# A two-layer decoder on one core: the FFN's down projection in two pairs of column blocks, with mixed pairs of row tiles

## The chip, the cores and the metric

The kernel runs on 1 core of one Trainium2 chip. The metric is the device time of one execution in microseconds (us). The kernel before takes 2395.1 us, the median of three runs (2394.01 to 2396.98).

## The reference

A state-space layer and a sliding-window attention layer, each followed by a SwiGLU feed-forward network (FFN), all in float32, 256 tokens of 2048 features. Around every part stand RMS norms. What this case changes is the FFN and the norm behind it, which run once in each of the two layers:

```
def rmsnorm(x, w):
    xf = x.astype(jnp.float32)
    xf = xf * lax.rsqrt(jnp.mean(xf * xf, axis=-1, keepdims=True) + EPS)
    return (xf * w.astype(jnp.float32)).astype(x.dtype)

def swiglu(u, w_gate, w_up, w_down):
    return (jax.nn.silu(u @ w_gate) * (u @ w_up)) @ w_down
...
        ffn = swiglu(rmsnorm(h, g[2]), ffn_w_gate[layer], ffn_w_up[layer], ffn_w_down[layer])
        h = h + rmsnorm(ffn, g[3])
```

`w_gate` and `w_up` are 2048 x 5632, `w_down` is 5632 x 2048.

## The kernel before

Every float32 product is made of three matmuls of fp32r tiles. A weight tile is loaded to `raw`, ACT casts it to a high half `whi` (line 113), DVE subtracts that from the raw tile and gets a low half `wlo` (line 114). The activations are kept as two halves in the same way. A product is then high x high, high x low and low x high, accumulated in one PSUM bank of 128 x 512.

The class `Weights` streams all weights in the order of one list, `specs`. It has five raw buffers and four buffers for converted halves; `next` converts up to three tiles ahead of the one that TensorE uses, and loads raw tiles ahead of that. A plain raw tile holds two row tiles of 128 x 512; its use is 12 matmuls (two row tiles, two token tiles, three matmuls). All loads of weights are issued on SP's queue.

Gate and up run in 11 units of 512 columns. From the second unit on, three of the eight pairs of row tiles are mixed. Gate and up stand side by side as a 2 x 2 block matrix (two row tiles, two column blocks), the two token tiles and two row tiles make a 2 x 2 block of activations, and their product is made with 7 products instead of 8. This needs sums of weight tiles (`_mixed`, lines 77 to 91, on DVE) and differences of activations (`mixed_x`, lines 624 to 635, once for each layer, kept in `sx`). The weights of a mixed pair come in four parts: "a" (two tiles as loaded), "13" (first sum, lines 87), "24" (second sums, lines 89 and 90, written into the raw tile in place) and "g" (one tile as loaded). The seven products collect in banks p1 to p7. When the last mixed pair is done, lines 696 to 700 recombine p1, p5, p6 and p7 into four stored terms, and lines 705 add them to the banks p2, p4, p3 and up1 at the unit's end; Silu and two products make a block of the hidden activations, which TensorE transposes during the next unit (line 641).

The down projection runs in `mix_stage` as four column blocks of 512, one after the other, with 22 plain raw tiles each. Behind a block ACT sums its squares and DVE multiplies by the norm's weights `gpost`, in the bank; all four blocks stay in the eight banks. The last block's final tiles are held (two in layer 0, four in layer 1) and run first for token tile 0, then for token tile 1. GpSimd makes the factor of the norm from the squares (line 240), and line 547 adds the scaled block to the residual `h`. `h` leaves the chip's SBUF for DRAM during the units (`spill_h`) and comes back through `fetch_h`, on GpSimd's queue, at the start of down.

The order on each engine is made by the framework's list scheduler from the order of the calls; `high_priority` moves a group ahead, `keep_in_program_order` pins it. The order on an engine is fixed when the kernel runs.

## Time and profile before

| | us |
|---|---|
| median of three runs | 2395.1 |
| the profiled execution | 2395.28 |
| its span, first to last instruction | 2393.6 |
| TensorE busy | 2371.8 |
| DVE busy | 1808.4 |
| ACT busy | 1322.2 |
| GpSimd busy | 92.0 |

Busy time of TensorE is a union of overlapping matmuls: a row of 0.39 us may start 0.23 us after the one before. In the lines of groups the first number after the bar is busy time in us, the second the mean duration in ns, then idle time of the engine before these instructions and what ended it. In a timeline the columns are start and duration in us, engine, line, operation, out<-in, shapes and count; in brackets stands the idle time before, with what ended it.

### The profile page before, as it was taken

How to read it: one execution, taken by the hardware profiler on the slowest of the kernel's cores; microseconds unless marked ns; L12 is line 12 of the kernel's file. 1: busy time of each engine (PE TensorE's matmuls, PEld its weight loads, DVE VectorE, ACT ScalarE, POOL GpSimd, SP SyncE). 2: the span in 40 equal slices, each digit the busy share in tenths (PEclk: the TensorE clock that was granted, in tenths of full speed). 3: DMA queues.
4: the chain of work that ended last, by engine and by line, in shares of the span. 5: the costliest groups of instructions: out<-in, count | busy, mean ns of one | idle time of the engine just before them, and what ended most of it. 6: DMA issues, size and time to landing. Idle time of an engine off the chain costs nothing.

```text
span 2393.6 us, 31662 instructions
## 1 busy us (share of the span) xinstructions
PE 2371.8 (99%) x11630; PEld 1963.9 (82%) x11630; DVE 1808.4 (76%) x2513; ACT 1322.2 (55%) x1867; POOL 92.0 (4%) x74
## 2 busy tenths in 40 slices
PE   9999999999999999999999999999999999999998
PEld 8888888888878888888888878777888888788887
DVE  6998878875567999999744468865899998894444
ACT  6666766664455555555544457755555555554443
POOL 2500100010000000000000000000000000000000
PEclk9999999999999999999999999999999999999999
DMA  7666666657665566565766664435565665566664
GB/s 224 182 202 191 192 186 193 187 174 245 194 199 193 181 202 211 187 213 175 270 193 194 194 192 151 129 123 184 189 210 181 207 211 178 200 230 225 193 194 142
DMA packets 287483, 462.19 MB, mean 193 GB/s; under 512 B 19024, under 2 KB 117584, under 8 KB 285536
## 3 DMA queue, kind: packets, MB, share of 16 engines
q1 hardware_dynamic: 285856, 451.39, 59.3%
q0 software_dynamic: 1184, 8.45, 0.9%
q8 instruction: 91, 1.49, 0.3%
q14 instruction: 64, 0.52, 0.1%
q10 hardware_dynamic: 288, 0.33, 0.0%
HBM read 453.76 MB, written 6.36 MB: 192 GB/s over the span
## 4 chain that ended last, share of the span: by engine, by line
PE 95%; ACT 2%; DVE 2%; issue 1%; DMA 0%; POOL 0%; DVEq 0%; SPq 0%; ACTq 0%; POOLq 0%
PE bank L286 14%; PE bank L345 12%; PE bank L346 12%; PE bank L344 12%; PE bank L669 11%; PE bank L670 11%; PE bank L668 11%; PE bank L291 8%; PE bank L641 1%; ACT whi L113 1%; DVE wlo L114 1%; PE bank L940 1%; PE bank L1116 1%; PE bank L1159 1%; PE bank L406 1%
## 5 line engine op out<-in xcount | busy, mean ns | idle before, releaser
L114 DVE TENSOR_TENSOR wlo<-raw,whi 128x1024 fp32r<-128x1024 f32 (+1 forms) x845 | 988.6, 1184 | 471.5 <-ACT whi L113 465.0
L113 ACT CAST whi<-raw 128x1024 fp32r<-128x1024 f32 (+1 forms) x845 | 853.7, 1022 | 790.4 <-PE bank L346 413.8
L286 PE MATMUL bank<-xx,whi 128*128 128x512 f32 (+1 forms) x1488 | 523.5, 397 | 0.0
L291 PE MATMUL bank<-xx,wlo 128*128 128x256 f32 (+1 forms) x1488 | 416.1, 285 | 0.0
L668 PE MATMUL bank<-whi,xx 128*128 128x512 f32 x980 | 385.2, 393 | 0.5 <-ACT whi L113 0.5
L669 PE MATMUL bank<-wlo,xx 128*128 128x512 f32 x980 | 382.2, 390 | 1.8 <-DVE wlo L114 1.8
L670 PE MATMUL bank<-whi,xx 128*128 128x512 f32 x980 | 382.3, 390 | 0.0
L286 PEld LDWEIGHTS bank<-xx,whi 128*128 128x128 f32 (+1 forms) x1488 | 276.6, 188 | 61.3 <-issue 0.4
L291 PEld LDWEIGHTS bank<-xx,wlo 128*128 128x128 f32 (+1 forms) x1488 | 280.3, 188 | 11.3 <-issue 7.0
L344 PE MATMUL bank<-whi,hh 128*128 128x512 f32 x704 | 274.2, 390 | 0.0
L346 PE MATMUL bank<-whi,hl 128*128 128x512 f32 x704 | 274.0, 389 | 0.0
L345 PE MATMUL bank<-wlo,hh 128*128 128x512 f32 x704 | 273.9, 389 | 0.0
L669 PEld LDWEIGHTS bank<-wlo,xx 128*128 128x128 f32 x980 | 184.1, 188 | 43.0 <-DVE wlo L114 5.4
L668 PEld LDWEIGHTS bank<-whi,xx 128*128 128x128 f32 x980 | 184.1, 188 | 38.1 <-ACT whi L113 0.9
L670 PEld LDWEIGHTS bank<-whi,xx 128*128 128x128 f32 x980 | 184.0, 188 | 37.9
L346 PEld LDWEIGHTS bank<-whi,hl 128*128 128x128 f32 x704 | 132.2, 188 | 27.5
L345 PEld LDWEIGHTS bank<-wlo,hh 128*128 128x128 f32 x704 | 132.2, 188 | 27.3
L344 PEld LDWEIGHTS bank<-whi,hh 128*128 128x128 f32 x704 | 132.2, 188 | 27.2
L113 ACT CAST whi<-t 128x1024 fp32r<-128x1024 f32 x60 | 63.2, 1054 | 90.6 <-DVE t L87 73.9
L344 PE MATMUL bank<-whi,yh 128*128 128x512 f32 x256 | 100.1, 391 | 0.0
L346 PE MATMUL bank<-whi,yl 128*128 128x512 f32 x256 | 99.7, 390 | 0.0
L345 PE MATMUL bank<-wlo,yh 128*128 128x512 f32 x256 | 99.6, 389 | 0.0
(215 smaller groups left out, 2868.1 us busy)
## 6 DMA issues: line engine op xcount, KB each, us to landing
raw<-in_ffn_w_down_dram SPq DMA_DIRECT2D x176, 512.0 KB, 4.8
raw<-in_ssm_w_in_dram SPq DMA_DIRECT2D x161, 512.0 KB, 4.4
raw<-in_ffn_w_gate_dram SPq DMA_DIRECT2D x116, 512.0 KB, 5.1
raw<-in_ffn_w_up_dram SPq DMA_DIRECT2D x116, 512.0 KB, 5.0
raw<-in_ssm_w_out_dram SPq DMA_DIRECT2D x64, 512.0 KB, 4.8
raw<-in_ffn_w_gate_dram SPq DMA_DIRECT2D x120, 256.0 KB, 3.8
raw<-in_ffn_w_up_dram SPq DMA_DIRECT2D x120, 256.0 KB, 4.2
raw<-in_attn_w_q_dram SPq DMA_DIRECT2D x32, 512.0 KB, 3.4
```

Source lines behind the costliest of these rows:

```text
L113: self.pin(nc.scalar.copy(hi[:], src))
L114: self.pin(nc.vector.tensor_tensor(lo[:], src, hi[:].bitcast(F32), ALU.subtract))
L286: nc.tensor.matmul(o, wh, xx[:, kt, :, :].rearrange("p a t -> p (a t)"), start=(kt == 0), stop=(kt == kts - 1))
L291: nc.tensor.matmul(o[:, :T], wl, xx[:, kt, 0, :], start=False, stop=False)
L344: nc.tensor.matmul(o, sh, wh, start=(kt == 0), stop=False)
L345: nc.tensor.matmul(o, sh, wl, start=False, stop=False)
L346: nc.tensor.matmul(o, sl, wh, start=False, stop=(kt == kts - 1))
L406: nc.tensor.matmul(o[:], hi[:, kk, cs], xr[2][:, kt, :, :].rearrange("p a t -> p (a t)"), start=(kt == 0), stop=(kt == KD - 1))
L641: nc.tensor.transpose(pt[:, P * k : P * (k + 1)], scr[:, NT + t, P * k : P * (k + 1)], ident[:])
L668: nc.tensor.matmul(o, sh, wh, start=(n == 1), stop=False)
L669: nc.tensor.matmul(o, sh, wl, start=False, stop=False)
L670: nc.tensor.matmul(o, sl, wh, start=False, stop=(n == total[name]))
```

## The change

The down projection now runs as two pairs of column blocks. In each pair the two blocks A and B take the places that gate and up have in a unit: the first pair has 6 mixed pairs of row tiles, the second 8. The class `Pairs` does this for units and down. The first pair's four results are kept in SBUF (`res`), already multiplied by the norm's weights and with their squares summed, and copied back to four banks near the end of the second. The differences of the hidden activations for eight mixed pairs are made once a layer, into `fx`, which takes the place of the layer's `xt`. `fetch_h` moves from the start of down to the place behind the second pair's last A tile, because `res` and the sums lie in the space before that.

In units and down, the parts of a mixed pair now come as "a", "g", "13", "24", the three sums are made together, in that order on DVE, in two tiles `t13` and `t24` of their own. The scratch tile of the squares has one buffer instead of two.

```diff
-S_ORDER = [3, 0, 4, 1, 5, 2, 6, 7]
...
+def down_order(npairs, lead, each, last_a):
+    rest = range(npairs, KF // SUB)
+    a_ = [("A", i) for i in rest]
+    b_ = [("B", i) for i in rest]
+    n = lead + each * npairs
+    na = len(a_) - last_a
+    subs = a_[:na] + b_[: n - na]
+    seq = subs[:lead]
+    for i in range(npairs):
+        seq += [("M", i)] + subs[lead + each * i : lead + each * (i + 1)]
+    return seq + [("E", 0)] + a_[na:] + b_[n - na :]
...
+UNIT = both(3) + [("M", 0)] + both(4) + [("M", 1)] + both(5) + [("M", 2), ("E", 0)] + both(6, 7)
+DOWN = [down_order(6, 8, 3, 4), down_order(8, 2, 2, 4)]
...
-                    for part in ("a", "13", "24", "g"):
+                    for part in ("a", "g", "13", "24"):
...
-        nc.vector.tensor_tensor(ta[:, 1, :], self.t13[:, 0, :], ta[:, 1, :], add)
-        nc.vector.tensor_tensor(ta[:, 0, :], ta[:, 1, :], tb[:, 0, :], add)
-        return ta[:]
+        if part == "24":
+            return self.t24[:]
+        t13, self.t24 = [self.spool.tile([P, 2, CW], F32, tag="t%d" % n, name="t%d" % n) for n in (13, 24)]
+        for o, p, q in ((t13[:], ta[:], tb[:, 1:2, :].broadcast_to([P, 2, CW])),
+                        (self.t24[:, 0, :], t13[:, 0, :], ta[:, 1, :]),
+                        (self.t24[:, 1, :], self.t24[:, 0, :], tb[:, 0, :])):
+            self.keep(nc.vector.tensor_tensor(o, p, q, add))
+        return t13[:]
...
-        for c in range(4):
-            add("down%d_%d" % (l, c), a["ffn_w_down"][l], KF, CW * c)
+        wd = a["ffn_w_down"][l]
+        for p in range(2):
+            add_pairs("down%d_%d" % (l, p), DOWN[p], (wd, 2 * CW * p), (wd, 2 * CW * p + CW))
...
+    def down_stage(layer, hid, todo, dp, close, lag):
+        mix = Mix(layer, 3)
+        fx = xtpool.tile([P, 8, 4, 2, P], F32R, tag="xx", name="fx")
+        res = dp.tile([P, 2, NT, CW], F32, tag="res", name="res")
...
+        def whole(c, t):
+            o = pp.bk[pp.OUT[2 * c + t]][:]
+            nc.vector.tensor_tensor(o, o, terms[2 * c + t], ALU.add)
+
+        def keep(c):
+            for t in range(NT):
+                src = pp.bk[pp.OUT[2 * c + t]][:]
+                mix.squares(src, c, t)
+                mix.post(res[:, c, t, :], src, c)
+
+        for p, made in ((0, range(6)), (1, range(6, 8))):
+            for i in made:
+                todo += [lambda i=i: make(i), None]
...
+                pp.item(item, terms)
...
+                if terms is not None and item[0] == "A" and order[n + 1][0] == "B":
+                    for t in range(NT):
+                        whole(0, t)
+                    if p == 0:
+                        keep(0)
+                    else:
+                        bks = [[bank() for _ in range(NT)] for _ in range(2)]
+                        for c in range(2):
+                            for t in range(NT):
+                                nc.scalar.copy(bks[c][t][:], res[:, c, t, :])
+                            mix.banks[c] = bks[c]
+                        mix.done([pp.bk[name] for name in pp.OUT[:2]], 2)
+                        mix.sums()
+                        close()
+                        fetch_h()
...
+        def products(t):
+            for (kind, i), (hi, lo, _, _) in held:
+                pp.rest(kind, i, hi, lo, ts=(t,))
+            with tc.high_priority():
+                whole(1, t)
+
+        mix.last([pp.bk[name] for name in pp.OUT[2:]], products)
+        return mix
...
             spool.__exit__(None, None, None)
-            fetch_h()
+            spool = tc.tile_pool(name="down%d" % layer, bufs=1, side="right")
+            W.spool = dp = spool.__enter__()
             todo += [None, lambda: store(FF // CW - 1)]
-            mix = mix_stage("down%d_" % layer, hid, KF, layer, 3, hook=hook, lag=2 if layer == 0 else CVB)
+            mix = down_stage(layer, hid, todo, dp, lambda: spool.__exit__(None, None, None),
+                             2 if layer == 0 else CVB)
```

On DVE, down of layer 0 was a row of low halves (`wlo`), with the products by `gpost` behind each block:

```order
L709 SCALAR_TENSOR_TENSOR scr<-vh,rs,scr 128x512 x2
L233 TENSOR_TENSOR hl<-bank,hh 128x4x128
L114 TENSOR_TENSOR wlo<-raw,whi 128x1024 x3
L233 TENSOR_TENSOR hl<-bank,hh 128x4x128 x2
L114 TENSOR_TENSOR wlo<-raw,whi 128x1024 x19
L503 TENSOR_TENSOR bank<-bank,gpost 128x512 x2
L114 TENSOR_TENSOR wlo<-raw,whi 128x1024 x22
```

The same engine in the changed kernel, at the third mixed pair of the first pair of blocks (line 113 makes sums, lines 662 and 665 sums and differences of activations in `yf`, line 262 the low half of `fx`):

```order
L137 TENSOR_TENSOR wlo<-raw,whi 128x512
L665 TENSOR_TENSOR yf<-yf 128x128 x3
L262 TENSOR_TENSOR fx<-yf,fx 128x4x128
L113 TENSOR_TENSOR t_10954<-raw 128x1024
L662 TENSOR_TENSOR yf<-hh,hl 128x512
L113 TENSOR_TENSOR t_10955<-t_10954,raw 128x512
L137 TENSOR_TENSOR wlo<-t_10954,whi 128x1024
L113 TENSOR_TENSOR t_10955<-t_10955,raw 128x512
L665 TENSOR_TENSOR yf<-yf 128x128 x4
L137 TENSOR_TENSOR wlo<-t_10955,whi 128x1024
L137 TENSOR_TENSOR wlo<-raw,whi 128x1024 x4
```

Between the sums and low halves of a mixed pair now stand the operations of a set of mixed inputs.

DVE at the head of a unit before (line 705 ends the unit before, 709 makes its products, 87 is the first sum of this unit's first mixed pair):

```order
L705 TENSOR_TENSOR scr<-bank,scr 128x512 x2
L87 TENSOR_TENSOR t_10158<-raw 128x1024
L114 TENSOR_TENSOR wlo<-raw,whi 128x1024
L705 TENSOR_TENSOR vh<-bank,vh 128x512 x2
L233 TENSOR_TENSOR hl<-bank,hh 128x4x128
L709 SCALAR_TENSOR_TENSOR scr<-vh,rs,scr 128x512 x2
L114 TENSOR_TENSOR wlo<-t_10158,whi 128x1024
L89 TENSOR_TENSOR raw<-t_10158,raw 128x512
L90 TENSOR_TENSOR raw<-raw 128x512
L114 TENSOR_TENSOR wlo<-raw,whi 128x1024
L114 TENSOR_TENSOR wlo<-raw,whi 128x512
```

and in the changed kernel:

```order
L844 TENSOR_TENSOR scr<-bank,scr 128x512 x2
L137 TENSOR_TENSOR wlo<-raw,whi 128x1024
L844 TENSOR_TENSOR vh<-bank,vh 128x512 x2
L848 SCALAR_TENSOR_TENSOR scr<-vh,rs,scr 128x512
L262 TENSOR_TENSOR hl<-bank,hh 128x4x128
L848 SCALAR_TENSOR_TENSOR scr<-vh,rs,scr 128x512
L137 TENSOR_TENSOR wlo<-raw,whi 128x512
L113 TENSOR_TENSOR t_10205<-raw 128x1024
L113 TENSOR_TENSOR t_10206<-t_10205,raw 128x512
L113 TENSOR_TENSOR t_10206<-t_10206,raw 128x512
L137 TENSOR_TENSOR wlo<-t_10205,whi 128x1024
L137 TENSOR_TENSOR wlo<-t_10206,whi 128x1024
```

The first sum moves from the place ahead of the products to the one behind them, the short low half of "g" ahead of it, and the three sums stand together.

TensorE at the end of layer 0's down, where the next stage begins with transposes of `h`, before:

```order
L344 MATMUL bank<-whi,hh 128x512
L345 MATMUL bank<-wlo,hh 128x512
L256 MATMUL bank<-ident,h 128x128 x4
L346 MATMUL bank<-whi,hl 128x512
L344 MATMUL bank<-whi,xx 128x512
```

and in the changed kernel:

```order
L693 MATMUL bank<-whi,hh 128x512
L694 MATMUL bank<-wlo,hh 128x512
L695 MATMUL bank<-whi,hl 128x512
L285 MATMUL bank<-ident,h 128x128 x4
L373 MATMUL bank<-whi,xx 128x512
```

The last matmul of down moves ahead of the first four transposes.

## Rows read from the trace of the kernel before

**Rows 1.** The page's first two parts: busy time of TensorE and DVE over the span, and in 40 equal slices the clock that TensorE was granted, in tenths of full speed.

```profile
PE 2371.8 (99%) x11630; PEld 1963.9 (82%) x11630; DVE 1808.4 (76%) x2513; ACT 1322.2 (55%) x1867; POOL 92.0 (4%) x74
...
PEclk9999999999999999999999999999999999999999
```

**Rows 2.** TensorE's matmuls in order of time in down of layer 0: the eight transposes behind the second tile with the matmul behind them, and, 88 matmuls apart, two near the end.

```profile
1172.79 1.04 PE L641 MATMUL bank<-ident,scr 128*128 128x128 f32 x8
1173.58 0.48 PE L344 MATMUL bank<-whi,hh 128*128 128x512 f32 x1
...
1384.74 0.39 PE L345 MATMUL bank<-wlo,hh 128*128 128x512 f32 x1
...
1404.69 0.39 PE L346 MATMUL bank<-whi,hl 128*128 128x512 f32 x1
```

**Rows 3.** Busy time by stretch: a unit of layer 0, and down of layer 0. Columns: stretch, length, then busy us and instructions of PE, PEld, DVE, ACT and POOL, granted clock, DMA share, GB/s.

```profile
1033.00:1075.00 42.00, 42.00 (x190) 34.64 (x188) 38.35 (x44) 23.83 (x27) 0.00 (x0) 1.00 0.58 194
1167.00:1400.00 233.00, 233.00 (x1036) 193.08 (x1035) 112.37 (x102) 95.19 (x101) 1.12 (x2) 1.00 0.65 206
```

**Rows 4.** One tile's conversion in down of layer 0, from the timeline of ACT and DVE.

```profile
1386.07 1.05 ACT L113 CAST whi<-raw 128x1024 fp32r<-128x1024 f32 x1 [1.67 <-PE bank L346]
...
1387.16 1.23 DVE L114 TENSOR_TENSOR wlo<-raw,whi 128x1024 fp32r<-128x1024 f32 x1 [1.50 <-ACT whi L113]
```

**Rows 5.** The head of a unit of layer 0, from the timeline of DVE, ACT and PE: the products of the unit before, the low half of "13", the last sum, its cast, the low half of "24" with four more, and the matmul that takes it; then the three sums of the next mixed pair and what follows.

```profile
828.49 1.41 DVE L709 SCALAR_TENSOR_TENSOR scr<-vh,rs,scr 128x512 f32<-128x512 f32 x2
829.81 1.22 DVE L114 TENSOR_TENSOR wlo<-t,whi 128x1024 fp32r<-128x1024 f32 x1
...
831.66 0.69 DVE L90 TENSOR_TENSOR raw<-raw 128x512 f32<-128x512 f32 x1
...
832.47 3.54 ACT L113 CAST whi<-raw 128x1024 fp32r<-128x1024 f32 x4 [4.62 <-DVE raw L90]
...
833.55 5.24 DVE L114 TENSOR_TENSOR wlo<-raw,whi 128x1024 fp32r<-128x1024 f32 x5 [1.19 <-ACT whi L113]
...
834.93 0.40 PE L669 MATMUL bank<-wlo,xx 128*128 128x512 f32 x1
...
838.70 1.22 DVE L87 TENSOR_TENSOR t<-raw 128x1024 f32<-128x1024 f32 x1
839.96 0.69 DVE L89 TENSOR_TENSOR raw<-t,raw 128x512 f32<-128x512 f32 x1
840.68 0.69 DVE L90 TENSOR_TENSOR raw<-raw 128x512 f32<-128x512 f32 x1
841.29 1.22 DVE L114 TENSOR_TENSOR wlo<-t,whi 128x1024 fp32r<-128x1024 f32 x1
```

**Rows 6.** Groups of DVE by line: the differences, sum and low half of a set of mixed inputs (from 706 to 780 us), and the additions at a unit's end (from 1033 to 1075 us).

```profile
L634 DVE TENSOR_TENSOR yf<-yf 128x128 f32<-128x128 f32 x12 | 3.0, 287 | 0.1
...
L631 DVE TENSOR_TENSOR yf<-xx 128x512 f32<-128x512 f32 x3 | 2.1, 689 | 0.1
L233 DVE TENSOR_TENSOR sx<-yf,sx 128x512 fp32r<-128x512 f32 x3 | 2.1, 687 | 0.9 <-ACT sx L232 0.9
...
L705 DVE TENSOR_TENSOR scr<-bank,scr 128x512 f32<-128x512 f32 x2 | 1.3, 682 | 0.0
```

**Rows 7.** TensorE's timeline at two third mixed pairs of units, one in each layer.

```profile
1110.15 0.39 PE L668 MATMUL bank<-whi,xx 128*128 128x512 f32 x1
1111.04 0.50 PE L669 MATMUL bank<-wlo,xx 128*128 128x512 f32 x1 [0.50 <-DVE wlo L114]
...
2086.51 0.39 PE L670 MATMUL bank<-whi,sx 128*128 128x512 f32 x1
2087.38 0.49 PE L668 MATMUL bank<-whi,xx 128*128 128x512 f32 x1 [0.49 <-ACT whi L113]
2088.64 0.50 PE L669 MATMUL bank<-wlo,xx 128*128 128x512 f32 x1 [0.77 <-DVE wlo L114]
```

**Rows 8.** The end of the kernel, from the timeline: the last matmul of down and the squares of its bank.

```profile
2384.97 0.39 PE L346 MATMUL bank<-whi,hl 128*128 128x512 f32 x1
2385.39 0.60 ACT L500 ACTIVATE junk<-bank 128x512 bf16<-128x512 f32 x1 [4.75 <-PE bank L346]
```

**Rows 9.** The end of layer 0, from the timeline: TensorE's last matmuls of down with the transposes between them, the first of the mask operations on GpSimd, and the factor of the second token tile behind them.

```profile
1407.18 0.39 PE L345 MATMUL bank<-wlo,hh 128*128 128x512 f32 x1
1407.94 0.66 PE L256 MATMUL bank<-ident,h 128*128 128x128 f32 x4 [0.37 <-DVE h L547]
1408.35 0.48 PE L346 MATMUL bank<-whi,hl 128*128 128x512 f32 x1
...
1408.97 0.43 POOL L1080 IOTA dm<- 128x128 f32 x2 [1.87 <-PE bank L346]
...
1411.27 0.54 POOL L240 TENSOR_TENSOR rs<-ms,neghalf 128x1 f32<-128x1 f32 x1
```

**Rows 10.** The view of DMA by issue: KB each and median us from issue to landing; last, of all moves of the residual, the least, median and greatest time to landing.

```profile
raw<-in_ffn_w_down_dram SPq DMA_DIRECT2D x176, 512.0 KB, 4.8
...
raw<-in_ffn_w_gate_dram SPq DMA_DIRECT2D x120, 256.0 KB, 3.8
...
h<-hd POOLq DMA_DIRECT2D x4, 1024.0 KB, 6.7
...
DMA to landing us min/median/max: 4.2/5.1/8.0
```

More of the change, by code (lines that the diff above doesn't have):

```diff
@@ L542, in mix_stage @@
-        return bks, rs
+        mix = Mix(layer, which)
+        for c in range(3):
+            if c == 0 and bk0 is not None:
+                bk = bk0
+            else:
+                bk = a_form("%s%d" % (key, c), xt, kts, hook=hook if c == 0 else None)
+            mix.done(bk, c)
+        mix.sums()
+        bk = [bank() for _ in range(NT)]
+        nsub = kts // SUB
+        held = []
+        for s in range(nsub):
+            hi, lo, _, per = W.next("%s%d" % (key, 3))
+            if s < nsub - lag:
+                for kk in range(per):
+                    a_mm(bk, xh, xl, hi, lo, kk, SUB * s + kk, kts, 0, CW)
+            else:
+                held.append((hi, lo, s, per))
```

281 lines of the change are left out of this document (158 added, 123 removed).

## The prediction

> **What bounds the kernel now.** I read the page's first two parts, then the matmuls one by one in time, then the busy time by stretch, and last the waits inside a unit, inside down and at the ends of the layers. TensorE is busy 99% of the span at the full clock, its higher level [rows 1]. That alone could mislead, since pipelined matmuls overlap, so the pace counts: in down, 88 starts lie between the two matmuls of [rows 2], 1404.69 - 1384.74 = 19.95 us, 0.2267 us each, back to back. Down holds no stall, and DVE is free for half of it, 112.4 of 233 us; in a unit DVE works 38.35 of 42 us [rows 3]. So a matmul that goes is worth 0.2267 us as long as DVE, which makes the low halves and the sums, keeps ahead. Four buffers hold converted weights, so DVE may be three tiles ahead and no more: in down each cast waits for TensorE to free one, and each low half waits 1.50 us for its cast [rows 4].
>
> **The change, part by part.**
>
> *Matmuls.* A mixed pair takes 7 products instead of 8, each of 3 matmuls. 14 pairs a layer, two layers: 14 x 2 x 3 = 84 matmuls of 512 columns fewer, x 0.2267 = 19.04 us. Nothing else is taken from TensorE or given to it.
>
> The Trainium skill ("TensorE: Matmul & The Clock Gate", Back-to-back issue gap) gives about 131 ns for each such matmul in a stream with weight loads; 84 of them would be worth 11.0 us, an estimate from that page. The row is of this very stream and decides; no chance is set aside for that figure.
>
> *DVE in the first pair of blocks.* A pair costs DVE three low halves of 1024, one of 512 and the three sums. In a row independent low halves start every 1.13 us (5.24 us for five, one of them short), and sums in a chain start 1.26 and 0.72 us apart [rows 5]: 3 x 1.13 + 0.60 + 1.26 + 0.72 + 0.61 = 6.6 us, against 21 x 0.2267 = 4.76 us on TensorE. A plain tile costs 1.13 against 12 x 0.2267 = 2.72. One set of mixed inputs is a sum, four short differences and a split, 0.69 + 4 x 0.287 + 0.69 [rows 6], 2.4 us with overlap. The order puts all eight sets into the first pair, the last two among the third and fourth mixed pair, though the second pair of blocks needs them. TensorE from the start of down to the last part of the sixth pair: 23 plain tiles and 6 pairs less one part, 62.6 + 28.6 - 1.4 = 89.8 us. DVE in that time: 20 low halves (three were ahead) 22.6, six pairs 39.6, eight sets 19.2, the end of the last unit 4.6 (two sums, two products, three splits [rows 5, 6]): 86.0, or 96%. It is tightest at the last part ("24") of the third pair: TensorE wants it after 14 plain tiles, two pairs and 16 matmuls, 38.1 + 9.5 + 3.6 = 51.2, and 0.8 for eight transposes [rows 2]; before it DVE has 11 low halves 12.4, three pairs 19.8, six sets and most of a seventh 16.1, and 4.6: 52.9. So about 0.9 late, and the handing of the last sum to ACT and back comes on top; I take 1.2 us a layer. Bounds: nothing, since the full buffers may cover it, and 1.67 us (the worst stall that a pair makes in before, 0.64 + 1.03 [rows 7]) at each of the four pairs that have sets beside them, 6.7 a layer.
>
> *DVE in the second pair.* Two plain tiles between pairs: 6.6 + 2 x 1.13 = 8.9 us of DVE for 4.76 + 5.44 = 10.2 of TensorE, the rhythm of a unit without its extra work. I take 0.5 a layer; bounds 0 and 1.7 (one such stall). The recombination, the four additions of stored terms and the four copies back lie behind the last mixed pair, where 10 plain tiles leave DVE and ACT more than half free: nothing. Banks: six are free when the second pair of blocks starts, and the seventh is wanted two plain tiles and 15 matmuls later, 8.8 us, while the two held ones need four DVE operations and two tiles' splits, some 5.
>
> *The units.* Same matmuls, casts and sums, in another order. Before, at the head of a unit, "24" was split from 833.55 to 834.77, and TensorE took it at 834.93: 0.16 us to spare; DVE had waited 1.19 us for the cast, because the sums were made after the split of "13" [rows 5]. Now the short tile "g" comes first, which gives TensorE three matmuls (0.68 us) to do, and the sums come in one go. From 829.81, where the products ended, DVE has 0.60 + 1.26 + 0.72 + 0.72 + 1.13 + 1.22 = 5.65 us up to 835.46; TensorE wants it at 834.93 + 0.68 = 835.61. That is 0.15 to spare, and up to 1.13 more, because the first sum no longer stands before those products. So no stall is added. The raw tiles come free at the last sum, not at the split behind it, so loads start earlier; the stalls of [rows 7] (distances of 0.89, 0.87 and 1.26 us, each less 0.23) are 0.66 + 0.64 + 1.03 = 2.3 us, all behind a low half or cast that was late. I take half as recovered, 1.2; bounds 0 and 2.3.
>
> *Ends of layers.* The addition of the stored term now stands between the last product and its square. Its nearest row, an addition of a bank and a stored term, is 0.682 us [rows 6]; with the handing on 0.75. At the kernel's end the square starts right behind the last matmul [rows 8], so it is all on the path: 0.75 (bounds 0.6 and 0.9). After layer 0 the first token tile's chain gets 0.75 later; but TensorE now has all its matmuls ahead of the transposes that wait for it, and GpSimd's nine mask operations, which begin at the last of these (1408.97) and hold the second token tile's factor until 1411.27 [rows 9], begin about 0.9 earlier (1408.35 less 1407.18 + 0.23). I take 0, bounds -0.7 and 0.8.
>
> *Transfers.* The residual is fetched only when the last A tile is added up, with six plain tiles to go: about 13.6 us until layer 0's first use (four tiles, then one half of two). Before, its two parts landed at a median of 6.7 us after the issue, at most 8.0 [rows 10]; some 3 us for additions and issue come ahead, so it is covered; layer 1 has 10.9 us (two tiles, one half of four) for the first part and 5.4 more for the second. On GpSimd's queue only the factors of the layer's end stand behind the fetch, and the weights of the norm keep their place on SP behind the same ten raw tiles. Not covered, a late landing would cost what it is late. Mixed pairs load 256 KB pieces, 3.8 us against 4.8 [rows 10]; the same bytes.
>
> Sum against the profiled execution of 2395.28 (span 2393.6 and 1.7 around it; median of the runs 2395.1, so the same to 0.01%): 2395.28 - 19.04 + 2 x (1.2 + 0.5) + 0.75 - 1.2 = 2379.2 us.
>
> **The rivals.**
>
> *DVE becomes the bound of the first pair of blocks.* For it: 96%, with no allowance for waits on ACT. Against: units at 91% run without a stall. With 1.67 us at four pairs of each layer, 0.5 in the second pair, and nothing recovered: 2395.28 - 19.04 + 13.4 + 1.0 + 0.75 = 2391.4; from half of that stall on, 2385 to 2391, 2388 as its mark. The Trainium skill ("VectorE: DVE Perf Modes", The DRAIN you can't avoid) speaks for it: an operation starts only when the one before has left the pipe, so the count of operations is what costs. With whole durations in place of distances the 86.0 above become 91.4, more than TensorE's 89.8. The rows show starts closer than durations between independent operations, so here the rule holds only for chains, of which the sums and sets are made.
>
> *The whole gain, and all old stalls gone.* For it: spare time at the head of a unit grows. 2395.28 - 19.04 + 0.75 - 2.3 = 2374.7.
>
> *The units pay for the new order.* 0.15 to spare is little: were each of five handings from one operation to the next 0.11 us (the cast behind a sum) above my distances, 0.4 us would be late in 20 units, 8 us: 2387.2. Against: the first sum's 1.13 us moved behind.
>
> *Slower.* Every mixed pair of down stalls for the split of "24", because its cast cannot start before the last sum, and its buffer comes free only three tiles ahead. The price is the wait that a unit shows for this, 1.19 us [rows 5], at 28 pairs: 33.3 us, 2395.28 - 19.04 + 0.75 + 33.3 = 2410.3. It decides from (19.04 - 0.75) / 28 = 0.65 us a pair on. Against: in the second pair of blocks DVE has 1.3 us to spare in each period.
>
> **How the numbers follow.** Forecast 0.60 (2375.5 to 2384), DVE-bound first pair 0.17, whole gain 0.11, units pay 0.07, slower 0.05. The range 2371 to 2389 leaves out the slower case, the upper part of the DVE-bound one, and what a faster tail would give. A run of this kernel tells 0.2% (4.8 us) from no change, so faster means under 2390.3: the forecast and the whole gain, 0.13 of the DVE-bound case, 0.06 of the units: 0.90. Same: 0.04 + 0.01, and 0.01 of a slower case that stays small: 0.06. Slower 0.04.
>
> **What would show it.** 84 matmuls fewer at an unchanged 0.2267 us; down some 8 us shorter in each layer (9.5 less 1.2 and 0.5); units as long as before or a little shorter; waits of TensorE for a low half at the third pair of each layer, and none from the fifth on; DVE busy over nine tenths in the first pair of blocks; the residual landed before its first use. Stalls at every pair of down, or a unit longer than before, would make the prediction wrong; so would a matmul pace other than 0.2267.

## The result and the profile after

The changed kernel takes 2377.38 us (median; 2377.05 to 2378.18) against 2394.82 us before: a ratio of 0.9926, 95% interval 0.9909 to 0.9943, so 17.4 us or 0.74% faster. Predicted were 2379.2 us, 2371 to 2389. The profiled execution took 2377.45 us, its span 2375.7.

The first two parts of the page, beside [rows 1]: TensorE has lost 84 matmuls and is still busy 99% at the full clock, and DVE has 168 us more to do. In the slices of both downs (21 to 24 and 37 to 40 of 40) DVE stands at 7 to 9 tenths, and at 6 in the very last.

```profile
PE 2353.2 (99%) x11546; PEld 1948.9 (82%) x11546; DVE 1976.5 (83%) x2781; ACT 1381.9 (58%) x1951; POOL 91.9 (4%) x74
...
DVE  6998887875567999999997878865899999999786
...
PEclk9999999999999999999999999999999999999999
```

Where the time went, by starts of matmuls in the two traces (us). The marks are the first transposes of hidden activations in a layer, which stand 36 us into its second unit, and the first and the last matmul of down; so "units" leaves out the first unit and most of the second.

| stage | before | after | difference | predicted |
|---|---|---|---|---|
| all up to the mark in the second unit | 777.64 | 778.59 | +0.95 | 0 |
| units from there, layer 0 | 389.58 | 388.36 | -1.22 | -1.2 for both layers |
| down, layer 0 | 241.13 | 232.41 | -8.71 | -7.8 |
| end of layer 0 up to the same mark in layer 1 | 345.11 | 345.59 | +0.48 | 0 (-0.7 to 0.8) |
| units from there, layer 1 | 391.35 | 388.36 | -2.99 | (above) |
| down, layer 1 | 240.16 | 233.05 | -7.11 | -7.8 |
| last matmul to the end | 8.61 | 9.37 | +0.77 | +0.75 |

The sum is -17.83, which is the difference of the two spans. Of the first row's 0.95 us, all lies ahead of the first use of a mixed input in the second unit (747.66 and 748.66), which the change does not aim at; in the 14 traces of this case that use comes between 747.66 and 749.0, so this is scatter. Without it the difference would have been about 1 us larger.

The pace of the matmuls, from TensorE's timeline, beside [rows 2]: these two starts lie 88 apart, (1395.06 - 1375.11) / 88 = 0.2267 us, as before.

```profile
1375.11 0.39 PE L693 MATMUL bank<-whi,hh 128*128 128x512 f32 x1
...
1395.06 0.39 PE L694 MATMUL bank<-wlo,hh 128*128 128x512 f32 x1
```

Busy time by stretch, beside [rows 3], in down of layer 0: its start up to the third mixed pair, and its two pairs of column blocks. DVE is busy for 49.3 of the first 52 us, 95%, and for 113.9 of 129 and 83.2 of 103 us in the two.

```profile
1166.95:1219.00 52.05, 52.05 (x236) 42.96 (x234) 49.30 (x79) 26.55 (x32) 0.00 (x0) 1.00 0.60 189
1166.95:1296.00 129.05, 128.40 (x569) 105.09 (x568) 113.85 (x151) 69.99 (x83) 0.00 (x0) 1.00 0.63 196
1296.00:1399.37 103.37, 103.37 (x458) 85.57 (x456) 83.23 (x91) 57.08 (x67) 1.54 (x3) 1.00 0.74 233
```

The first of two places where TensorE still waits in down: the third mixed pair, at its part "24", in both layers. The timeline of DVE and ACT first, then TensorE's.

```profile
1213.95 1.22 DVE L113 TENSOR_TENSOR t<-raw 128x1024 f32<-128x1024 f32 x1
1215.09 0.69 DVE L662 TENSOR_TENSOR yf<-hh,hl 128x512 f32<-128x512 f32 x1
1215.69 0.68 DVE L113 TENSOR_TENSOR t<-t,raw 128x512 f32<-128x512 f32 x1
...
1217.51 0.69 DVE L113 TENSOR_TENSOR t<-t,raw 128x512 f32<-128x512 f32 x1
...
1218.31 1.05 ACT L136 CAST whi<-t 128x1024 fp32r<-128x1024 f32 x1 [1.97 <-DVE t L113]
...
1218.80 0.39 PE L695 MATMUL bank<-whi,fx 128*128 128x512 f32 x1
1219.41 0.50 PE L693 MATMUL bank<-whi,fx 128*128 128x512 f32 x1 [0.22 <-ACT whi L136]
...
1220.36 0.73 PE L693 MATMUL bank<-whi,hh 128*128 128x512 f32 x2 [0.22 <-ACT whi L136]
```

Between the sums (L113) stands the head of a set of mixed inputs (L662), and the end of another, which waited 0.69 us for ACT, ran up to the first of them. So the last sum ends late, ACT casts it at 1218.31, and TensorE, which could have started at 1219.03, starts at 1219.41; it waits for the cast, not for a low half. With a second wait and the slower starts behind both that is 1.05 us, in layer 1 (at 2185.77) 1.05 again.

The second place is the head of the second pair of blocks. DVE's timeline in layer 1 first, then TensorE's:

```profile
2245.65 1.22 DVE L113 TENSOR_TENSOR t<-raw 128x1024 f32<-128x1024 f32 x1 [2.94 <-DMA raw<-in_ffn_w_down_dram]
2246.80 1.22 DVE L137 TENSOR_TENSOR wlo<-raw,whi 128x1024 fp32r<-128x1024 f32 x1
2247.93 1.29 DVE L744 TENSOR_TENSOR bank<-bank,res 128x512 f32<-128x512 f32 x2
2249.13 0.68 DVE L113 TENSOR_TENSOR t<-t,raw 128x512 f32<-128x512 f32 x1
...
2256.19 0.68 DVE L113 TENSOR_TENSOR t<-t,raw 128x512 f32<-128x512 f32 x1
...
2260.79 0.50 PE L694 MATMUL bank<-wlo,fx 128*128 128x512 f32 x1 [0.48 <-DVE wlo L137]
```

The first sum of the first mixed pair stands ahead of a plain low half and of the additions of stored terms (L744), and DVE stood 2.94 us until that sum's weights had landed. The three sums are not together here: the third starts 7.06 us behind the second, with two additions, four products by `gpost` and three low halves between them. DVE is then late 15 us on: 1.23 us for TensorE here, and 0.54 in layer 0, where the same sum waited 1.85 us.

The wait alone does not make the stall. In the run with three mixed pairs in the first pair of blocks (below) the same sum waits as long, 1.97 us in layer 0 and 2.01 in layer 1, and no stall follows. There half of the additions and products lie elsewhere, and the other two sums come at once behind the plain low half:

```profile
2249.39 1.23 DVE L113 TENSOR_TENSOR t<-raw 128x1024 f32<-128x1024 f32 x1 [2.01 <-DMA raw<-in_ffn_w_down_dram]
...
2251.67 1.41 DVE L113 TENSOR_TENSOR t<-t,raw 128x512 f32<-128x512 f32 x2
```

No unit holds a stall any more. The residual, fetched at 1384.85 and 2351.86, landed in 7.2 us at the median; its first uses on DVE stand 14.7 and 12.0 us behind these issues and wait for no load.

The kernel's end, beside [rows 8]: the addition of the stored term is on the path, 0.43 + 0.79 us from the last matmul to the square, where it was 0.42.

```profile
2366.37 0.39 PE L695 MATMUL bank<-whi,hl 128*128 128x512 f32 x1
2366.80 0.70 DVE L744 TENSOR_TENSOR bank<-bank,gpost 128x512 f32<-128x512 f32 x1 [0.24 <-PE bank L695]
2367.59 0.60 ACT L531 ACTIVATE junk<-bank 128x512 bf16<-128x512 f32 x1 [4.75 <-DVE bank L744]
```

And the end of layer 0, beside [rows 9]: all matmuls of down now precede the transposes. The mask operations end ahead of the second token tile's factor, which no longer waits for them but 0.23 us for its mean square on DVE (L267). It starts 3.05 us behind the last matmul, where it was 2.92. But before, the last matmul itself stood behind four transposes, 0.94 us after its place in the pace (1408.35 against 1407.18 + 0.23). Counted from that place the factor comes 0.81 us earlier than before. The wait of TensorE for the second token tile's residual, 0.78 us before, is gone; for the first token tile it now waits 0.60 and 1.26 us, where it was 0.37 and 0.44. A row of before that [rows 9] does not have:

```profile
1412.65 1.09 PE L256 MATMUL bank<-ident,h 128*128 128x128 f32 x8 [0.78 <-DVE h L547]
```

and of the changed kernel:

```profile
1399.37 0.39 PE L695 MATMUL bank<-whi,hl 128*128 128x512 f32 x1
...
1401.89 0.29 POOL L1223 TENSOR_SCALAR_AFFINE_SELECT dm<-dm 128x128 f32<-128x128 f32 x1
1402.42 0.54 POOL L269 TENSOR_TENSOR rs<-ms,neghalf 128x1 f32<-128x1 f32 x1 [0.23 <-DVE ms L267]
```

So 0.94 of the 8.71 us in the table's row of layer 0's down belong to the end of the layer: without them down is 7.77 us shorter, and the stretch behind it 0.46 shorter instead of 0.48 longer. Counted so, that stretch takes 345.5 to 346.1 us in the four traces with the old down, and 345.6 to 345.7 in the three with the new one in which TensorE's clock does not fall there (last section), so it is the same within their scatter.

### The profile page after: what moved, and what is told of

The parts are those of the page before. It is cut to its first block, busy times and chain, and to the rows that moved or that the text cites. A ratio compares the mean times of both kernels' runs of the same rounds, so it can differ in the third digit from the quotient of the medians.

```text
span 2375.7 us, 32156 instructions
## 1 busy us (share of the span) xinstructions
PE 2353.2 (99%) x11546; PEld 1948.9 (82%) x11546; DVE 1976.5 (83%) x2781; ACT 1381.9 (58%) x1951; POOL 91.9 (4%) x74
## 4 chain that ended last, share of the span: by engine, by line
PE 96%; DVE 1%; ACT 1%; DMA 1%; issue 0%; SPq 0%; DVEq 0%; POOL 0%; ACTq 0%; POOLq 0%
PE bank L695 17%; PE bank L694 17%; PE bank L693 17%; PE bank L315 14%; PE bank L320 8%; PE bank L373 5%; PE bank L375 5%; PE bank L374 5%; PE bank L823 1%; DMA raw<-in_ffn_w_down_dram 1%; DVE wlo L137 1%; PE bank L1081 1%; PE bank L1257 1%; PE bank L1300 1%; PE bank L435 1%
## 5 line engine op out<-in xcount | busy, mean ns | idle before, releaser
L137 DVE TENSOR_TENSOR wlo<-raw,whi 128x1024 fp32r<-128x1024 f32 (+1 forms) x785 | 890.4, 1162 | 220.0 <-ACT whi L136 212.9
L136 ACT CAST whi<-raw 128x1024 fp32r<-128x1024 f32 (+1 forms) x785 | 776.5, 1005 | 464.5 <-PE bank L695 203.0
L136 ACT CAST whi<-t 128x1024 fp32r<-128x1024 f32 x176 | 185.6, 1055 | 330.7 <-DVE t L113 228.9
L137 DVE TENSOR_TENSOR wlo<-t,whi 128x1024 fp32r<-128x1024 f32 x176 | 215.1, 1222 | 66.5 <-ACT whi L136 65.3
L694 PE MATMUL bank<-wlo,hh 128*128 128x512 f32 x564 | 219.8, 390 | 0.4 <-DVE wlo L137 0.4
L693 PE MATMUL bank<-whi,hh 128*128 128x512 f32 x564 | 219.8, 390 | 0.4 <-ACT whi L136 0.4
L695 PE MATMUL bank<-whi,hl 128*128 128x512 f32 x564 | 219.6, 389 | 0.0
L113 DVE TENSOR_TENSOR t<-t,raw 128x512 f32<-128x512 f32 x176 | 121.6, 691 | 5.3
L693 PEld LDWEIGHTS bank<-whi,hh 128*128 128x128 f32 x564 | 105.7, 188 | 23.1 <-ACT whi L136 1.3
L113 DVE TENSOR_TENSOR t<-raw 128x1024 f32<-128x1024 f32 x88 | 107.3, 1220 | 5.9 <-DMA raw<-in_ffn_w_down_dram 5.9
```

Of the source, the lines that this page charges most:

```text
L113: self.keep(nc.vector.tensor_tensor(o, p, q, add))
L136: self.pin(nc.scalar.copy(hi[:], src))
L137: self.pin(nc.vector.tensor_tensor(lo[:], src, hi[:].bitcast(F32), ALU.subtract))
L693: nc.tensor.matmul(o, s[0], wh, start=(n == 1), stop=False)
L694: nc.tensor.matmul(o, s[0], wl, start=False, stop=False)
L695: nc.tensor.matmul(o, s[1], wh, start=False, stop=(n == self.total[name]))
```

## The experiments

Each was timed against the kernel before on the same chip, in five rounds. In the first four the question is which part of the change is worth what.

**Only the units new** (the kernel before, with the units' mixed pairs in the new order and with the new sums, held in their place; the two products of "24" swapped and one buffer for the squares, both as in the changed kernel; down old).

```diff
-                    for part in ("a", "13", "24", "g"):
+                    for part in ("a", "g", "13", "24"):
...
+        t13, self.t24 = [self.spool.tile([P, 2, CW], F32, tag="t%d" % n, name="t%d" % n) for n in (13, 24)]
...
+            self.keep(nc.vector.tensor_tensor(o, p, q, add))
```

> The kernel before, with only the mixed pairs of the units changed (parts a, g, 13, 24, the three sums together, in tiles of their own); down as it was. Theory 1: the 4.2 us by which the two traces' units differ (1.2 in layer 0, 3.0 in layer 1) come from this part, so 2394.8 - 4.2 = 2390.6 us, and no stall of TensorE over 0.3 us in any unit. Theory 2: the stalls of the kernel before were chance of its one profile (loads that landed late), so no difference, 2394 to 2396. The prediction's own term was 1.2 us: 2393.6.

Measured 2391.83 us, ratio 0.9988 (0.9979 to 0.9997). The units of both layers last 388.36 us, -1.22 and -2.99, exactly as in the changed kernel, and down is as before. So the units' part stands by itself. The time is between the two theories: over all executions the gain is 2.6 us (2394.41 to 2391.83), where the two profiled ones differ by 3.9. So the 4.2 us belong to these traces; by the medians the units' part is worth less.

**The new order alone** (the kernel before; sums written over the first tiles, each ahead of its own part, as they were).

```diff
-                    for part in ("a", "13", "24", "g"):
+                    for part in ("a", "g", "13", "24"):
```

> The kernel before, with the parts of a unit's mixed pair in the new order, but the sums still in the raw tile and each ahead of its own part. Theory 1a: the order does it, because the short part gives TensorE 0.68 us of work while the first sum is cast: 2390.6 us. Theory 1b: the tiles do it, because raw tiles come free sooner: no gain, 2394 to 2396. If both count, in between.

Measured 2400.28 us, 1.0027 (1.0017 to 1.0036): slower, which neither theory had. The units lose 4.15 and 1.98 us. DVE and TensorE at one head of a unit:

```profile
835.24 0.68 DVE L90 TENSOR_TENSOR raw<-raw 128x512 f32<-128x512 f32 x1
837.12 2.36 DVE L114 TENSOR_TENSOR wlo<-raw,whi 128x1024 fp32r<-128x1024 f32 x2 [1.19 <-ACT whi L113]
...
838.40 0.50 PE L669 MATMUL bank<-wlo,xx 128*128 128x512 f32 x1 [0.66 <-DVE wlo L114]
```

The wait of 1.19 us of [rows 5] is still there, behind the last sum. With "g" ahead the other parts come no earlier on DVE, and the low half of "24" is late.

**The new sums alone** (as the run with only the units new, but order a, 13, 24, g).

```diff
+        t13, self.t24 = [self.spool.tile([P, 2, CW], F32, tag="t%d" % n, name="t%d" % n) for n in (13, 24)]
...
+            self.keep(nc.vector.tensor_tensor(o, p, q, add))
```

> The kernel before, with the three sums of a unit's mixed pair together and in tiles of their own, but the parts in the old order (a, 13, 24, g). Theory 1a (order): little gain, 2393 to 2396. Theory 1b (tiles): the loads start at the last sum and not after the split behind it, the stalls go, 2390.6 us. A stall at the head of each unit would show that the old order needs the first sum early.

Measured 2391.50 us, 0.9988 (0.9980 to 0.9997), the units -1.23 and -2.99. So the sums, with the place held, give all of the units' gain. DVE at the same head of a unit: the sums, then the two low halves of their tiles, without a wait.

```profile
829.80 1.21 DVE L91 TENSOR_TENSOR t<-raw 128x1024 f32<-128x1024 f32 x1
831.05 1.42 DVE L91 TENSOR_TENSOR t<-t,raw 128x512 f32<-128x512 f32 x2
832.38 2.50 DVE L115 TENSOR_TENSOR wlo<-t,whi 128x1024 fp32r<-128x1024 f32 x2
```

**The new down with the old sums and order** (the changed kernel; sums written over the first tiles, their place on DVE not held).

```diff
-            self.keep(nc.vector.tensor_tensor(o, p, q, add))
+            self.t13 = self.spool.tile([P, 2, CW], F32, tag="t13", name="t13")
...
+        nc.vector.tensor_tensor(ta[:, 1, :], self.t13[:, 0, :], ta[:, 1, :], add)
+        nc.vector.tensor_tensor(ta[:, 0, :], ta[:, 1, :], tb[:, 0, :], add)
```

> The changed kernel, with the old order of parts and the old sums (in the raw tile, each ahead of its own part) in units and in down. If the gain of the change is matmuls alone, 2377.4 us plus the units' 4.2: 2381.6. If down needs the new sums as well, each of its 28 mixed pairs loses up to the 1.19 us for which DVE waited for a cast in a unit, so up to 33 us more: 2382 to 2415; my mark is 2388, a quarter of that.

Measured 2417.71 us, 1.0098 (1.0084 to 1.0112): 23 us slower than before, 40 slower than the changed kernel, and past the range. Down takes 252.81 and 250.16 us. DVE and TensorE at one mixed pair:

```profile
1304.84 1.23 DVE L109 TENSOR_TENSOR t<-raw 128x1024 f32<-128x1024 f32 x1 [3.56 <-DMA raw<-in_ffn_w_down_dram]
...
1310.99 2.96 DVE L136 TENSOR_TENSOR wlo<-raw,whi 128x1024 fp32r<-128x1024 f32 x3 [1.19 <-ACT whi L135]
...
1312.27 0.51 PE L693 MATMUL bank<-wlo,hh 128*128 128x512 f32 x1 [0.76 <-DVE wlo L136]
```

Two waits of DVE at one pair: the first sum stands ahead of plain work and waits 3.56 us for its load (25.7 us over the 14 pairs of layer 0), and the low half of "24" waits 1.19 us for its cast. So the mixed pairs of down do not pay with these sums.

The next four change where DVE's work lies in down.

**The last two sets beside light work** (made behind the first pair's last mixed pair, beside six plain tiles, held there).

```diff
-        for p, made in ((0, range(6)), (1, range(6, 8))):
+        for p, made in ((0, range(6)), (1, range(0))):
...
+                        todo += [lambda: make(6), None, lambda: make(7), None]
```

> The changed kernel, but the last two sets of mixed inputs are made beside the six plain tiles behind the first pair of blocks' mixed pairs, and not between its third and fifth mixed pair. Theory (DVE's load ahead of the third mixed pair, and in the second pair of blocks a sum of weights that was moved ahead of plain work and waits for its load there, make the stalls): the 1.0 us at the third pair of each layer goes, and of the 0.5 and 1.2 us at the head of the second pair most goes as well: 2377.4 - 2.0 - 1.7 = 2373.7. Rival (the head of the second pair of blocks stalls whatever stands ahead of it): only the 2.0 us goes, 2375.4. Rival (the third pair stalls for its own loads or for ScalarE, not for the sets): no change, 2377.4.

Measured 2374.11 us, 0.9917 (0.9904 to 0.9931): the theory's figure to 0.4 us. Down takes 230.72 and 230.73 us and holds no stall at a mixed pair. That is 4.0 us less than in the changed kernel, a little more than the theory's 3.7; 1.3 us are lost again behind layer 0's down, where the clock falls (last section). At the head of the second pair of blocks, in layer 1, the additions and the plain low halves now come ahead of the first sum, which waits for nothing:

```profile
2248.88 1.29 DVE L745 TENSOR_TENSOR bank<-bank,res 128x512 f32<-128x512 f32 x2
...
2251.93 1.22 DVE L113 TENSOR_TENSOR t<-raw 128x1024 f32<-128x1024 f32 x1
```

**The last two sets in the second pair** (held where they are written, ahead of its first two mixed pairs).

```diff
+                    tc.keep_in_program_order if i > 5 else lambda ins: ins)
```

> The changed kernel, but the last two sets stay where they are written, behind plain work of the second pair of blocks' head, ahead of its first two mixed pairs. Theory (a set beside a mixed pair costs TensorE what DVE is late): the 1.0 us at the third pair goes in each layer, and 2.4 us of DVE's work for a set comes ahead of a pair that has two plain tiles before it, with 1.3 us to spare in each such period: about 1 us of stall for each of the two, so 2377.4 - 2.0 + 2 x 2 x 1 = 2379. Rival (DVE is three tiles ahead there, and takes two sets in its stride): 2375.4.

Measured 2381.53 us, 0.9948 (0.9935 to 0.9960). The stall of the third pair is gone, and the first two pairs of the second pair of blocks stall, 1.83 us each instead of the 1 expected (TensorE, layer 0):

```profile
1291.07 0.73 PE L693 MATMUL bank<-whi,fx 128*128 128x512 f32 x2 [0.57 <-ACT whi L136]
1292.53 0.50 PE L693 MATMUL bank<-whi,fx 128*128 128x512 f32 x1 [0.72 <-ACT whi L136]
```

The sets carry the stall with them. (Of the 2.5 us over the theory's 2379, 1.6 lie behind layer 0's down, as in the run above.)

**Eight mixed pairs in the first pair of blocks**, two plain tiles between them.

```diff
-DOWN = [down_order(6, 8, 3, 4), down_order(8, 2, 2, 4)]
+DOWN = [down_order(8, 6, 2, 4), down_order(8, 2, 2, 4)]
...
-        for p, made in ((0, range(6)), (1, range(6, 8))):
+        for p, made in ((0, range(8)), (1, range(8, 8))):
```

> The changed kernel with eight mixed pairs in the first pair of blocks too, instead of six. Two pairs a layer more take 2 x 2 x 3 = 12 matmuls, 2.7 us. Theory (DVE has no time left in the first pair of blocks, 96% by the working): the two pairs cost about what they save, and the stalls of the third pair grow by 0.5 to 1.5 us a layer: 2376 to 2378. Rival (DVE still keeps up, since it is ahead by the fifth pair): 2374.7. Rival (the DVE is the bound there already): two pairs and their sums want 2 x (6.6 - 4.76) = 3.7 us a layer more of DVE than of TensorE, 2382 and over.

Measured 2381.32 us, 0.9945 (0.9932 to 0.9959): the rival, nearly. 12 matmuls fewer, and 4 us more than the changed kernel: 2.25 in the two downs, 1.9 behind layer 0's down, where the clock falls. DVE is busy for 10.9 of 1231.41 - 1220.23 = 11.18 us a period, where TensorE has 10.2 to do:

```profile
1220.23 1.23 DVE L137 TENSOR_TENSOR wlo<-t,whi 128x1024 fp32r<-128x1024 f32 x1 [0.26 <-ACT whi L136]
1221.37 4.09 DVE L137 TENSOR_TENSOR wlo<-raw,whi 128x1024 fp32r<-128x1024 f32 x4
...
1231.41 1.23 DVE L137 TENSOR_TENSOR wlo<-t,whi 128x1024 fp32r<-128x1024 f32 x1 [0.26 <-ACT whi L136]
```

The working of the prediction gives 6.6 for a pair, 2 x 1.13 for two plain tiles and 2.4 for a set, 11.26 us.

**Three mixed pairs in the first pair of blocks** (`down_order(3, 8, 3, 4)`).

> The changed kernel with three mixed pairs in the first pair of blocks instead of six. Three pairs fewer a layer are 18 matmuls more in all, 4.1 us. Theory (each of the pairs left out was worth its whole 0.68 us, and only one of them stalled for 1.0 us a layer): 2377.4 + 4.1 - 2 x (0 to 1.0) = 2379.5 to 2381.5. Rival (the pairs of the first pair of blocks bring nothing, DVE being the bound there): 2377.4.

Measured 2380.34 us, 0.9942 (0.9929 to 0.9954), in the theory's range. Down takes 233.78 and 234.03 us. The stall of the third pair, here the last, stays (1.0 and 1.3 us), and the second pair of blocks has none. Take these stalls away, and down is 2.04 us longer than the stall-free one of the run with the sets beside light work, 9 matmuls: each pair left out was worth its 0.68 us. 1.3 us of the run's time are again those behind layer 0's down, so that the range is hit owes something to luck.

The last four ask what in the new sums counts, and whether there is more.

**The new sums in the old order**, in the units and in down.

```diff
-                    for part in ("a", "g", "13", "24"):
+                    for part in ("a", "13", "24", "g"):
```

> The changed kernel with the new sums (all three together, in tiles of their own), but the four parts of a mixed pair in the old order: first tiles, then the two sum tiles, and the short tile last, in the units and in down. Theory (what counts is where the sums stand on DVE, since the units gained as much in the old order): 2377.4, at most 1 us from it. Rival (the short tile gives TensorE 0.68 us to do while the sums are made, which the units do not need and down does, where DVE has little left): a stall of 0.3 to 0.7 us at the 28 pairs of down, 2386 to 2397.

Measured 2375.42 us, 0.9921 (0.9907 to 0.9934): 2 us under the changed kernel, against the rival and more than the theory allowed. Down is 231.19 and 231.32 us, 1.2 and 1.7 less than in the changed kernel: the stall at the third pair is half as long, and none is left at the head of the second pair of blocks, where the first sum does not wait. So the new order brings nothing: with the new sums it costs a little in down, and with the old ones it harms the units.

**The sums apart**: own tiles, their place held, but the first sum ahead of the split of "13" and the others behind it.

```diff
+        if part == "13":
+            self.keep(nc.vector.tensor_tensor(self.t13[:], ta[:], tb[:, 1:2, :].broadcast_to([P, 2, CW]), add))
+            return self.t13[:]
```

> The changed kernel in its new order and with the sums in tiles of their own, but not in one go: the first sum ahead of the split of '13', the other two behind it, ahead of the split of '24'. Theory (the one go is what counts: behind the split of '13' the two sums, the cast and the split of '24' stand in a row, with a wait of DVE for the cast of 1.19 us that a unit showed): stalls of 0.5 to 1.4 us at nearly every mixed pair of down and at some of the units, 2392 to 2418. Rival (the tiles of their own are what counts, since raw buffers and first tiles no longer wait for sums written over them): 2377.4 to 2380.

Measured 2474.18 us, 1.0335 (1.0320 to 1.0349): the theory's way and far past its range. DVE and TensorE at the head of a unit:

```profile
790.26 1.22 DVE L109 TENSOR_TENSOR t<-raw 128x1024 f32<-128x1024 f32 x1
792.67 1.23 DVE L137 TENSOR_TENSOR wlo<-t,whi 128x1024 fp32r<-128x1024 f32 x1 [1.19 <-ACT whi L136]
793.81 1.41 DVE L113 TENSOR_TENSOR t<-t,raw 128x512 f32<-128x512 f32 x2
796.41 1.23 DVE L137 TENSOR_TENSOR wlo<-t,whi 128x1024 fp32r<-128x1024 f32 x1 [1.19 <-ACT whi L136]
...
796.43 0.50 PE L693 MATMUL bank<-whi,sx 128*128 128x512 f32 x1 [1.26 <-ACT whi L136]
```

Sum, cast, low half, sums, cast, low half: a chain in which DVE stands 1.19 us twice, 66.5 us over the units of layer 0. From the first mixed pair to the start of down they grow by 36.3 against before. Down, with its 42 matmuls fewer (9.5 us), is still 3.4 and 4.4 us longer than before, so it stalls by about 1 us a pair, as the theory had it; the units, where the theory saw stalls only in some, stall in each, by about 2.0, 1.0 and 0.4 us at their three pairs. In one go, the cast of "13" runs beside the other two sums, and that of "24" beside the low half of "13".

**The sums apart and free**: the same, their place not held.

> As the kernel with the sums apart in tiles of their own (2474.2), but their place on DVE is not held: the scheduler may move them ahead of or behind other work, as it may in the kernel with in-place sums (2417.7) and as it may not in the changed kernel. Theory (both 1.19 us waits in a row for a cast, with nothing between them, are what made 2474, and holding the sums apart in their place is what leaves nothing between): the sums move among plain low halves, the stalls of the units go or nearly, and it comes out like the in-place sums or better, 2385 to 2418. Rival (sums apart in tiles of their own are bad in themselves, since raw buffers come free later and loads come late): 2440 and over. Rival (the tiles of their own are all that counts once the scheduler is free): 2377.4, at most 2 us from it.

Measured 2441.24 us, 1.0192 (1.0178 to 1.0206). The number is the rival's, the place is not: the units, at 391.5 and 394.4 us, have lost nearly all stalls of the run before, as the theory had it, and down takes 263.5 and 257.3. DVE's groups by line there say why:

```profile
L109 DVE TENSOR_TENSOR t<-raw 128x1024 f32<-128x1024 f32 x14 | 17.1, 1225 | 33.8 <-DMA raw<-in_ffn_w_down_dram 33.8
```

The 14 first sums stand ahead of plain work and wait 33.8 us for their loads. With the same tiles and the place held these waits were 2.5 us, so it is the place, and not the tiles, that makes the loads late for them. What the new sums are without their place held was not tried in one go.

**Seven mixed pairs in the first pair of blocks**, behind eleven plain tiles, on top of the sets beside light work (`down_order(7, 11, 2, 4)`).

> The variant with the last sets beside light work (2374.1), now with seven mixed pairs in the first pair of blocks, behind eleven plain tiles and with two plain tiles each; the eighth set alone is made behind them. One pair a layer more saves 6 matmuls, 1.36 us in all. Theory (a period of two plain tiles and a pair holds 10.2 us of TensorE and 8.9 of DVE without a set, 11.3 with one; five to six of the seven sets are made ahead of the first pair, one or two beside pairs): 0 to 1.2 us of stall a layer, so 2372.7 to 2375, 2373 as the mark. Rival (eleven plain tiles with their sets are already as long on DVE as on TensorE, and no lead is left at the first pairs): stalls of about 1 us at three pairs or more of each layer, 2378 and over.

Measured 2375.14 us, 0.9920 (0.9906 to 0.9933), just over the theory's range. Down is 231.22 and 231.28 us: 1.36 us of matmuls less in all, and three stalls of 0.25 us with their slower starts in each layer more than eat them. By the medians the best version is that with six pairs and the sets beside light work; the intervals of the two overlap, and it is the traces of down that tell them apart.

The addition of the stored terms ahead of the last matmuls, which might save the 0.75 us at the kernel's end, was not tried.

## Why the prediction was right

*The sum.* 2379.2 said, 2377.4 measured. The matmuls, the third pair and the addition at the end came out as said; the units gave 3.0 us more than said in the two traces, and 0.95 us of scatter at the start hid a part of that.

*Matmuls.* 84 fewer, at 0.2267 us: as the working had it, 19.04 us, and the three pairs less of one run and the stall-free down of another (10.40 and 9.42 us shorter than before, for 9.52 of matmuls and, in layer 0, the transposes that no longer stand between the last matmuls) agree.

*The first pair of blocks.* 1.2 us a layer were said, for the part "24" of the third mixed pair; 1.05 were measured, there, in both layers. That DVE's sets cause it is shown by the two runs that moved them; the new order of the parts has a share, since in the old one the stall is half as long. The size is in part luck: the working had 52.9 us of DVE's work in 52.0 of TensorE's up to there, and left out all waits for ACT but the last; in the trace DVE is busy 49.3 us and waits 2.6 us for casts. Up to the last part of the sixth pair DVE was to need 86.0 of 89.8 us, 96%; the trace has 84.1 of 91.9, 92%. The DVE-bound rival was near: with eight pairs it is the case.

*The second pair.* 0.5 a layer were said, 0.54 and 1.23 measured. The size is near by luck, since the reason was not in the working: it counted DVE's time, and left out both that a sum may stand ahead of work that is ready, where it waits for a load, and that the additions and products of the first pair may stand between the sums. It takes both: with the wait and half of the additions there is no stall (three pairs), and with all of them and no wait there is none either (sets beside light work).

*The units.* Said -1.2 with a bound of -2.3, measured -4.21: the term that was mis-sized. Two things failed. The step took half of the old stalls as recovered, while all went. And [rows 7] shows three, where the trace of before has a fourth, 0.71 us at 2001.83. With about 0.1 us of slower starts behind three of the stalls that is 3.4 us; the other 0.8 are 0.04 us a unit in the pace, from no single wait. Over the executions of the run with only the units new the gain is less, 2.6 us, a little over the bound. The comparison of the order had it that "g" ahead gives TensorE 0.68 us to spare; the runs say that this counted for nothing, and that the sums did it.

*The ends.* 0.75 said, 0.77 measured at the kernel's end. From the end of layer 0 to the next units 0.48 by the table, -0.46 when the 0.94 us of the mark are put where they belong; both lie within the bounds of -0.7 to 0.8, and the traces of the other runs show no difference beyond scatter. The gain from earlier mask operations, which was to pay for the addition, came: the factor is 0.81 us earlier, counted from where the matmuls would have ended.

*The rival on the slower side* was real, and the way the sums are made kept it away. It priced 1.19 us at each of the 28 pairs, 33.3 us; with the old sums the pairs of down cost (252.81 - 230.72) / 14 = 1.58 and (250.16 - 230.73) / 14 = 1.39 us against the stall-free down, and the kernel is 23 us slower than before. What the prediction put against it, spare time of DVE in each period, does not tell the two apart: DVE is busy for 197.0 us in down of layer 0 in both kernels. The order of a few operations does, and whether it is held.

*Distances against durations.* The Trainium skill ("VectorE: DVE Perf Modes", The DRAIN you can't avoid) has each operation start when the one before has left the pipe. The same section adds that a next operation that is not held starts earlier, which the prediction left out, and that is what the trace shows: by whole durations the period of the run with eight pairs would be some 11.9 us; it is 11.18, with low halves of 1.23 us that start 1.13 us apart. So the distances decided here.

## What to carry to other kernels

Before work is shifted onto an engine that has time, draw the chain through the other engine that each piece needs: where a sum is cast elsewhere and comes back, make all sums first, so that the casts run beside them. Hold a sum in its place if a scheduler could put it ahead of ready work, since it then stands in line until its load lands; with the sums apart this cut the waits from 33.8 to 2.5 us in one down. It is no guarantee: the changed kernel's sums are held, and one still waited 2.94 us. And place side work by period (6.6 + 2 x 1.13 + 2.4 against 10.2 us), beside the stretch where the bounding engine has plain work, rather than by its share of the whole stage.

## What the runs showed of the hardware

A wait can cost more than its length, through TensorE's clock. In the run with the sums apart and free, behind a wait of 3.33 us the matmuls start 0.43 us apart, and the stretch behind it has a granted clock of 0.50, that is 1.2 instead of 2.4 GHz, where those before and after have 1.00. TensorE's timeline, then busy time by stretch:

```profile
1215.69 0.80 PE L694 MATMUL bank<-wlo,fx 128*128 128x512 f32 x1 [3.33 <-DVE wlo L137]
1216.29 0.63 PE L695 MATMUL bank<-whi,fx 128*128 128x512 f32 x1
1216.71 0.63 PE L693 MATMUL bank<-whi,hh 128*128 128x512 f32 x1
```

```profile
1200.00:1211.90 11.90, 11.90 (x54) 9.86 (x53) 9.57 (x16) 6.21 (x8) 0.00 (x0) 1.00 0.68 219
...
1215.70:1221.80 6.10, 6.10 (x14) 4.78 (x15) 5.17 (x5) 1.04 (x1) 0.00 (x0) 0.50 0.48 137
1221.80:1232.00 10.20, 10.20 (x46) 8.45 (x45) 6.85 (x13) 5.70 (x7) 0.00 (x0) 1.00 0.55 177
```

The same fall stands behind the waits at the end of layer 0 in the run with the sets beside light work, not in the changed kernel, whose waits there are alike (0.60 and 1.26 us). The 0.60 in this row is a mean over 4 us; in its slow part matmuls start 0.43 us apart (1401.42, 1401.85, 1402.28):

```profile
1401.00:1405.00 4.00, 4.00 (x15) 3.24 (x16) 2.48 (x4) 1.21 (x3) 0.00 (x0) 0.60 0.00 0
```

The stretch from the last matmul of down to the first product with the attention's output takes 153.74 us there, 152.15 in the changed kernel: 1.6 us, without which that run would be near 2372.5, an estimate.

The traces of six more runs show this fall at this place: sets in the second pair, eight, three and seven pairs, the new sums in the old order, and the sums apart. Those of the changed kernel, of the old sums in the new down, and of the sums apart and free do not. Leaving out the sums apart, where the mark of the units lies elsewhere, the table's row from the end of layer 0 to the units of layer 1 is 346.7 to 347.5 us with the fall and 345.6 to 345.7 without. So where such a run is compared with the changed kernel, 1.1 to 1.9 us of its time are not its edit's, as far as its other executions are like the traced one. Why the clock falls in some and not in others stays open.
